# Moving nine depthwise-convolution taps of the second layer from VectorE to ScalarE, GpSimd and transfers

## The chip, the cores and the metric

The kernel runs on one core of a Trainium2 chip. The metric is the device time of one execution in microseconds. Before the change it is 2174.63 us, the median of three runs (2174.32 to 2175.8).

The engines, by the names that the profile uses: PE is TensorE (PEld its weight loads), DVE is VectorE, ACT is ScalarE, POOL is GpSimd and SP is SyncE, which issues transfers. Each engine runs its own instructions in the order in which they stand in the program, and waits on semaphores for the others.

## What is computed

An encoder trunk of two layers on 1024 tokens of width 1024, in float32. Each layer runs multi-head latent attention and a Conformer convolution side by side on the same normalised input, projects both back, and then runs a gated feed-forward block with a short convolution. Cut to what matters here:

```python
for l in range(DEPTH):                                   # DEPTH = 2
    h = _rmsnorm(x, g_mix[l])
    p = h @ w_in[l]
    c_q = _rmsnorm(p[..., :o1], g_q[l])                  # 384 wide
    q = (c_q @ w_uq[l]).reshape(b, s, 8, 96)
    c_kv = _rmsnorm(p[..., o1:o2], g_kv[l])              # 256 wide
    kv = (c_kv @ w_ukv[l]).reshape(b, s, 8, 128)
    k_rope = _apply_rope(p[..., o2:o3], cos, sin)        # 32 wide, shared by the heads
    y_attn = _mla_attention(q_nope, q_rope, k_nope, k_rope, v)
    a, gt = jnp.split(p[..., o3:], 2, axis=-1)
    u = a * jax.nn.sigmoid(gt)                           # 512 channels
    u = _dwconv(u, w_dw_conv[l], b_dw_conv[l])           # 31 taps
    u = jax.nn.silu(_layernorm(u, g_conv_ln[l], b_conv_ln[l]))
    x = x + jnp.concatenate([y_attn, u], axis=-1) @ w_o[l]
    ...                                                  # gated feed-forward block
```

`_dwconv` is the part that the change touches: for each of 512 channels, 31 shifted copies of `u`, each times a weight of its channel, are added up.

## The kernel before

Channels lie on the 128 partitions and tokens along the free dimension, so the 512 channels of the convolution are four blocks j = 0 to 3 of 128 x 1024. For each block there is a tile `gate` (which holds `u` after the gating) and a tile `conv`, in which the sum is built. One tap is one product of a shifted part of `gate` with a column of `par`, added to `conv`. The middle tap starts the sum on ACT (L693). The other 30 taps of a block are done in one of three ways:

- **near taps**, on DVE: one SCALAR_TENSOR_TENSOR multiplies and adds (L2164). `NEAR_TAPS` says how many of each block are of this kind.
- **far taps**: ACT multiplies into a tile `far` (L2170), and a transfer that POOL issues adds this tile to `conv` (L2171, 511.5 KB).
- **late taps**, during attention: POOL multiplies into a tile `late` (L2181) and either a transfer adds it (L2186) or, for every fifth, POOL itself does (kind "both", L2184). Whatever is neither near nor far becomes late.

A layer has three parts: `project`, `attention` and `feed`. `project` walks through sections of matmuls, each of which fills one PSUM bank pair: the gates and values g0, a0 to g3, a3, the key-value latents kv0 and kv1, the shared rotary key kr, the query latents q0 to q2, and from the normalised latents the keys k0 to k3, the rotary queries u0 and u1 and the other queries n0 to n3. The order of what DVE and ACT do beside them is decided while the program is written, by a model clock. After each section the clock moves on by that section's estimate, and then: if the section is longer than 5.0 us, up to `FAR_TOGETHER` far taps are put out, from blocks whose last far tap lies `FAR_GAP` = 8.0 us back; `work` fills DVE's modelled time with near taps of 1.28 us and with the steps of the evictions; and the section's own eviction is launched. So a near tap stands wherever the model saw room on DVE, and far taps stand on ACT between a section's matmuls and its eviction.

The steps of `project` that matter below, by line:

- L226 and L227 (`complete`): ACT negates a loaded weight (`wu11h` into `wu11l`), and POOL adds the original to it by a transfer, which leaves what the rounding lost. L211 is POOL's load of that weight.
- L219: ACT scales the weight of a q section.
- L756 to L771 (`key_rope`): the shared key, in turn on ACT (L756), DVE (L758, L764, L765), ACT (L768), DVE (L770) and ACT (L771).
- L304, L315 to L323, L342: the sum of squares of a latent is turned by PE, reduced and brought to a root on DVE, and turned back by PE. The key latent's root is named `rkv1`, the query's `rq1`.
- L714, L724 (`latent`): ACT brings a query latent out of PSUM into `cq` and squares it.
- L778, L780 (`key_rope_end`): the shared key split in two halves, `krs`, by ACT and DVE.
- L790, L792 (`parts`): the high half (ACT) and the low half (DVE) of a normalised latent, `kvs` or `cqs`.
- L802, L804 (`key`): the same for a key section, `ks`, out of PSUM; L804 is the last reader of its bank.
- L265: the matmuls of the sections.

Three PSUM bank pairs are used in turn, so k3 writes the bank that k0 used, k0 that of q1 and k2 that of q2. SBUF tiles of tag "b" (31 slots of 128 x 1024) take the slots that came free, whichever tile had them before; an instruction that writes a tile waits for the last reader of the slot's former one. The tiles `far` of the second layer are of tag "ws" (8 slots).

In attention each block of work goes to a step by number (`agenda`). The late taps are spread over the steps in proportion to their modelled cost. On POOL, between them, stand the heads' normalisation (`yt`, L2037), two halves `ys_1l` and `ys_3l` (L247) and at the end the sum over the four blocks (`lns`, L2192).

Of the kernel before, what the change touches and what calls it, by code (L numbers as in the profile page):

```python
# [88 lines left out]
MANUAL = [E.PE, E.DVE, E.Activation, E.Pool, E.SP]  # L89
LATE_KINDS = (("pool", "both", "pool", "pool", "pool"), ("pool", "both", "pool", "pool", "pool"))  # L90
LATE_COST = {"act": 1.1, "pool": 2.7, "both": 4.1}
NEAR_TAPS = (12, 14, 15, 14)
NEAR_ORDER = (0, 1, 2, 3)
FAR_TOGETHER = 3
FAR_GAP = 8.0
# [52 lines left out]
class Encoder:  # L148
# [442 lines left out]
    def project(self, l, carry):  # L591
# [3 lines left out]
        taps, active, u, conv, away, far_at = [], [], {}, {}, {}, {}  # L595
# [17 lines left out]
        def out_squares(now):  # L613
            while outs and outs[0][0] <= now:
                at, i, t = outs.pop(0)
                if t is None:
                    outs.append((at + OUT_WAIT, i, self.out_rows(l, i, "b")))
                    outs.sort(key=lambda e: e[0:2])
                else:
                    nc.scalar.activation(out=t, in_=t, func=AF.Square, accum_out=sc[:, 3 + i:4 + i])  # L620
# [19 lines left out]
        def work(until):  # L640
            while True:
                at = next((e for e in active if e[0] <= clock["dve"]), None)
                if at is None and taps and clock["dve"] + TAP <= until:
                    j, t = taps.pop(0)
                    self.conv_step(l, j, u[j], conv[j], t)
                    clock["dve"] += TAP
                    continue
                if at is None:
                    at = min(active, key=lambda e: e[0], default=None)
                    if at is None or at[0] > until:  # L650
                        return
                    clock["dve"] = max(clock["dve"], at[0])
                step = next(at[1], None)
                if step is None:
                    active.remove(at)
                else:
                    clock["dve"] += step[0]
                    at[0] = clock["dve"] + step[1]

        def launch(steps, n=-1):  # L660
            active.append([clock["pe"], steps, n])

        def finish(n):
            for e in [e for e in active if e[2] <= n]:
                for step in e[1]:
                    clock["dve"] = max(clock["dve"], e[0]) + step[0]
                    e[0] = clock["dve"] + step[1]
                active.remove(e)
# [17 lines left out]
        def glu(j):  # L686
            g = u[j] = gates.pop(j)
            if l:
                nc.vector.scalar_tensor_tensor(out=g, in0=ps[f"a{j}"], scalar=by, in1=g, op0=ALU.mult, op1=ALU.mult)
            else:  # L690
                nc.vector.tensor_tensor(out=g, in0=ps[f"a{j}"], in1=g, op=ALU.mult)
            y = conv[j] = self.blk(f"conv{l}_{j}")
            nc.scalar.activation(out=y, in_=g, func=AF.Identity, scale=self.tap(l, j, PAD),  # L693
                                 bias=par[:, P_BC + j:P_BC + j + 1])
            yield 1.22, 1.5
            todo = [t for t in range(KC) if t != PAD]
            taps.extend((j, t) for t in todo[:NEAR_TAPS[j]])
            taps.sort(key=lambda e: NEAR_ORDER.index(e[0]))
            away[j] = todo[NEAR_TAPS[j]:]
            far_at[j] = 0.0  # L700

        def tables():
# [188 lines left out]
        def last_gate():  # L891
            yield from glu(1)
            yield from tables()

        add("a1", "a1", inputs("a1"), last_gate)
        for j in (2, 3):
            add(f"g{j}", f"g{j}", inputs(f"g{j}"), lambda j=j: gate(j))
            add(f"a{j}", f"a{j}", inputs(f"a{j}"), lambda j=j: glu(j))
# [18 lines left out]
        times, starts, t = {}, {}, 0.0  # L917
# [12 lines left out]
        def supply(now, turn=TURN):  # L930
            for name, at in [e for e in coming if e[1] <= now + LEAD + ahead(e[0])]:
                coming.remove((name, at))
                turning.append((name, at, self.cast(l, name, "b" if l else "ws")))
            for name, at, e in [e for e in turning if e[1] <= now + turn + ahead(e[0])]:
                turning.remove((name, at, e))
                if l and name in BLOCKS:
                    e = self.scaled(*e)
                    w[name] = e[0]
                    launch(rest_of(e), st.get("n", -3) - 2)
                    continue  # L940
                w[name] = self.complete(*e)
                if name == "k":
                    head_squares(name)
# [4 lines left out]
        launch(gate(0), -3)  # L948
        work(clock["pe"] + 6.0)
        launch(glu(0), -2)  # L950
        launch(gate(1), -1)
        for n, (name, weight, emit, evict, after) in enumerate(seq):
            st["n"] = n
            supply(clock["pe"])
            out_squares(clock["pe"])
            finish(n - 3)
            if l and name == "q2":
                self.banks[0][0].append(self.banks[0][0].pop(0))
            ps[name] = self.wide(f"p{name}{l}")
            emit()  # L960
            clock["pe"] += times[name]
            queue = [i for i, _ in taps]
            far = [j for j in away if clock["pe"] >= far_at[j] and
                   (j not in queue or queue.count(j) == NEAR_TAPS[j] and queue.index(j) > 8)]
            for j in sorted(far, key=far_at.get)[:FAR_TOGETHER if times[name] > 5.0 else 0]:
                self.tap_far(l, j, away[j].pop(0), u[j], conv[j])
                far_at[j] = clock["pe"] + FAR_GAP
            work(clock["pe"])
            if after:
                after()  # L970
            launch(evict(), n)
            if l and (name[0] == "q" or name[:2] == "kv"):
                active[-1][0] += next(active[-1][1])[1]
# [1355 lines left out]
```

## Time and profile before

| | before |
|---|---|
| median of 3 runs | 2174.63 us |
| the profiled execution | 2174.99 us |
| its span, first instruction to last | 2173.2 us |
| busy share PE, DVE, ACT, POOL | 99%, 86%, 68%, 24% |
| near taps (L2164), both layers | 110, 1274 ns each |
| far taps (L2171), both layers | 31 |
| late taps (L2181), both layers | 99, 1356 ns each |

The page's rows on the busy slices of the span:

```profile
PE   9999999999999999999999999999999999999998
DVE  6989999879998887887978889998898988878877
PEclk9999999999999999999999999999999999999999
```

Each digit is the busy share of a fortieth of the span, in tenths, 9 for 90% or more; PEclk is the granted TensorE clock in the same way. The second layer's projections begin about 1120 us and end about 1283; attention follows to about 1466.

In a timeline row stand the start in us, the duration, the engine, the line, the operation, what it writes and reads, how many instructions the row groups, and in brackets how long the engine was idle before it and what ended that.

### The profile page before, as it was taken

To read this page: it belongs to the slowest core of one execution; us is meant where nothing else is said; L and a number is where in the kernel's file an instruction comes from. 1 tells how busy PE (TensorE), PEld (TensorE's weight loads), DVE (VectorE), ACT (ScalarE), POOL (GpSimd) and SP (SyncE) were. 2 spreads that over 40 slices of the span, in tenths; PEclk is the share of its full clock that TensorE was granted. 3 is DMA by queue.
4 is the path that set the end of the run, shared out by engine and by line. 5 is a ranking of instruction groups with operands and counts; after the bars stand their busy time and mean duration, and the time that the engine had idled before them with its cause. 6 is when DMAs were issued, how large, how long until landed. Compare 5 with 4: busy or idle time off the path is not lost. (4 is left out here: it accounts for less than half of the span.)

```text
span 2173.2 us, 29821 instructions
## 1 busy us (share of the span) xinstructions
PE 2160.0 (99%) x10726; PEld 1178.4 (54%) x10726; DVE 1858.7 (86%) x2558; ACT 1479.5 (68%) x2208; POOL 515.8 (24%) x506
## 2 busy tenths in 40 slices
PE   9999999999999999999999999999999999999998
PEld 8887666754444444444444576667544444444445
DVE  6989999879998887887978889998898988878877
ACT  6455888746898889554534668886478888865544
POOL 1233767211211111000001256771111111110000
PEclk9999999999999999999999999999999999999999
DMA  6898878855689898555345776786646988856533
GB/s 193 184 188 211 167 146 168 256 150 118 140 239 260 225 289 262 190 173 186 115 160 115 170 186 138 158 193 194 175 102 160 263 241 241 243 136 220 187 115 122
DMA packets 161220, 400.95 MB, mean 184 GB/s; under 512 B 19840, under 2 KB 27888, under 8 KB 161072
## 3 DMA queue, kind: packets, MB, share of 16 engines
q1 hardware_dynamic: 104080, 266.79, 35.8%
q0 software_dynamic: 56704, 131.74, 33.6%
q8 instruction: 84, 1.38, 0.3%
q14 instruction: 64, 0.52, 0.1%
q10 hardware_dynamic: 288, 0.53, 0.1%
HBM read 270.75 MB, written 69.66 MB: 157 GB/s over the span
## 5 line engine op out<-in xcount | busy, mean ns | idle before, releaser
L1384 PE MATMUL p<-b,w 128*128 128x512 f16 x3696 | 800.3, 379 | 0.2
L1384 PEld LDWEIGHTS <-w 128*128 128x128 f16 x3696 | 358.8, 98 | 431.7 <-issue 0.8
L1658 PE MATMUL pd<-ab,wd 128*128 128x512 f16 (+1 forms) x1920 | 401.0, 371 | 0.4 <-DVE ab L1648 0.4
L1260 POOL DMA_DIRECT2D wu<-in_w_up x176 | 151.8, 876 | 771.0 <-DVE w L1348 584.8
L1658 PEld LDWEIGHTS <-wd 128*128 128x128 f16 x1920 | 187.9, 98 | 210.7 <-issue 0.9
L1943 PE MATMUL s<-k,q 96*128 96x512 f16 x768 | 186.9, 379 | 0.0
L1348 DVE SCALAR_TENSOR_TENSOR w<-wu,wf,w 128x512 f16<-128x512 f32 (+1 forms) x216 | 177.1, 833 | 5.4 <-ACT w L1345 5.4
L1986 DVE SCALAR_TENSOR_TENSOR pt<-t,pt 128x512 f16<-128x512 f32 x256 | 162.9, 676 | 10.1 <-ACT pt L1985 9.1
L1345 ACT ACTIVATE w<-wu,wf 128x512 f16<-128x512 f32 (+1 forms) x216 | 164.9, 781 | 0.7 <-DMA wu<-in_w_up 0.7
L1985 ACT ACTIVATE pt<-t 128x512 f16<-128x512 f32 x256 | 139.1, 596 | 31.9 <-PE t L1983 30.0
L1945 DVE TENSOR_REDUCE mx<-s 128x1 f32<-128x1024 f32 x128 | 154.9, 1210 | 0.9 <-PE s L1943 0.9
L1647 ACT ACTIVATE ab<-ac,ds 128x512 f16<-128x512 f32 x108 | 75.5, 716 | 110.8 <-DVE ac L1553 76.2
L1953 ACT ACTIVATE p<-s,mx 128x1024 f32<-128x1024 f32 x128 | 143.3, 1119 | 2.2 <-DVE mx L1945 1.8
L2164 DVE SCALAR_TENSOR_TENSOR conv<-gate,par,conv 128x1009 f32<-128x1009 f32 (+14 forms) x110 | 139.7, 1274 | 2.8 <-ACT conv L693 0.2
L2181 POOL TENSOR_SCALAR late<-gate,par 128x1012 f32<-128x1012 f32 (+14 forms) x99 | 134.2, 1356 | 29.7 <-PE pn L265 29.7
L1983 PE MATMUL t<-ident,p 128*128 128x128 f32 x1024 | 136.6, 275 | 0.9 <-ACT p L1953 0.6
L1983 PEld LDWEIGHTS t<-ident,p 128*128 128x128 f32 x1024 | 116.8, 141 | 34.9 <-issue 7.4
L1891 DVE SCALAR_TENSOR_TENSOR o<-zg,par,o 128x1023 f32<-128x1023 f32 x88 | 112.6, 1280 | 10.0 <-ACT o L1885 8.4
L1891 DVE SCALAR_TENSOR_TENSOR v<-zv,par,v 128x1023 f32<-128x1023 f32 x88 | 112.1, 1276 | 1.4 <-ACT v L1885 1.4
L1392 DVE SCALAR_TENSOR_TENSOR zg<-p,wf,zg 128x512 f32<-128x512 f32 x72 | 54.0, 749 | 66.7 <-PE p L1384 53.0
L1943 PEld LDWEIGHTS <-q 96*128 96x128 f16 x768 | 74.1, 97 | 64.5 <-issue 2.1
L2171 POOL DMA_DIRECT2D conv<-far x31 | 27.3, 901 | 333.4 <-ACT far L2170 321.3
(1536 smaller groups left out, 3708.0 us busy)
## 6 DMA issues: line engine op xcount, KB each, us to landing
wu<-in_w_up SPq DMA_DIRECT2D x98, 512.0 KB
wu<-in_w_up POOLq DMA_DIRECT2D x176, 256.0 KB, 5.1
sd<-in_w_down SPq DMA_DIRECT2D x44, 512.0 KB
ws<-sd SPq DMA_DIRECT2D x44, 512.0 KB
act<-v SPq DMA_DIRECT2D x36, 512.0 KB
ac<-act SPq DMA_DIRECT2D x72, 256.0 KB
wo<-in_w_o POOLq DMA_DIRECT2D x32, 256.0 KB, 7.8
x_mix<-y SPq DMA_DIRECT2D x32, 256.0 KB
```

What stands on the lines that cost most here:

```text
L1260: nc.gpsimd.dma_start(out=dst, in_=src, accum_op=ALU.add)
L1345: nc.scalar.activation(out=t, in_=src, func=AF.Copy, scale=scale[f])
L1348: nc.vector.scalar_tensor_tensor(out=t, in0=src, scalar=scale[f], in1=hi, op0=ALU.mult, op1=ALU.subtract)
L1384: nc.tensor.matmul(ps, w[p][:, k * 128:(k + 1) * 128], b[:, q], start=(i in (1, 5, 2) and k == 0 and t == 0), stop=(k == 3 and t == 2), sk ...
L1658: nc.tensor.matmul(ps[t, m][:, cs], w[i, j][p][:, m * 128:(m + 1) * 128], b[:, q, cs], start=(i in (1, 5, 2) and j == 0 and s == 0), stop= ...
L1891: self.nc.vector.scalar_tensor_tensor(out=o[:, a:b], in0=z[:, at + a:at + b], scalar=self.par[l][:, tap:tap + 1], in1=o[:, a:b], op0=ALU.m ...
L1943: nc.tensor.matmul(ps[:, cs], q[0:96, i, qs], k[0:96, j, cs], start=(s == 0), stop=(s == 2))
L1945: nc.vector.tensor_reduce(out=mx, in_=ps, op=ALU.max, axis=AX.X, negate=True)
L1953: nc.scalar.activation(out=p, in_=ps, func=AF.Exp, bias=mx, accum_out=st["sums"][:, qt:qt + 1])
L1983: nc.tensor.transpose(tp[:, i, qi * 128:(qi + 1) * 128], st["p"][2 * qp + qi][:, kt * 128:(kt + 1) * 128], self.ident)
L1986: nc.vector.scalar_tensor_tensor(out=lo, in0=tp, scalar=P_SCALE, in1=hi, op0=ALU.mult, op1=ALU.subtract)
L2164: self.nc.vector.scalar_tensor_tensor(out=y[:, lo:hi], in0=u[:, lo + s:hi + s], scalar=self.tap(l, j, t), in1=y[:, lo:hi], op0=ALU.mult, o ...
```

## The change

Only numbers change: `NEAR_TAPS` becomes a tuple per layer. The first layer keeps 12, 14, 15 and 14; the second has 9, 11, 13 and 13, nine fewer. In the second layer up to four far taps follow a long section instead of three. Since far taps are put out in more and larger groups, five more taps are far there (16 before, 21 now), and the remaining four become late (49 before, 53 now).

```diff
-NEAR_TAPS = (12, 14, 15, 14)
+NEAR_TAPS = (12, 14, 15, 14), (9, 11, 13, 13)
...
-            taps.extend((j, t) for t in todo[:NEAR_TAPS[j]])
+            taps.extend((j, t) for t in todo[:NEAR_TAPS[l][j]])
...
-            away[j] = todo[NEAR_TAPS[j]:]
+            away[j] = todo[NEAR_TAPS[l][j]:]
...
-                   (j not in queue or queue.count(j) == NEAR_TAPS[j] and queue.index(j) > 8)]
-            for j in sorted(far, key=far_at.get)[:FAR_TOGETHER if times[name] > 5.0 else 0]:
+                   (j not in queue or queue.count(j) == NEAR_TAPS[l][j] and queue.index(j) > 8)]
+            for j in sorted(far, key=far_at.get)[:FAR_TOGETHER + l if times[name] > 5.0 else 0]:
```

The order of PE's and SP's instructions stays as it is. What moves on the others is shown at three places of the second layer's `project`. A far tap's name carries its block and its tap: `far_2_16` is tap 16 of block 2.

First ACT, from the weight wu01 to the start of the shared key, around section kr. Before:

```order
L226 ACTIVATE wu01l<-wu01h 128x768
L2170 ACTIVATE far_2_16_10612<-gate_2_10261,par_155 128x1023
L219 ACTIVATE wq2s<-wq21r,wz 128x1024
L226 ACTIVATE wu11l<-wu11h 128x768
L2170 ACTIVATE far_0_17_10672<-gate_0_10052,par_155 128x1022
L2170 ACTIVATE far_1_17_10675<-gate_1_10114,par_155 128x1022
L2170 ACTIVATE far_2_17_10678<-gate_2_10261,par_155 128x1022
L756 ACTIVATE krt_10682<-pkr_10579,wz 64x1024
```

The same place after:

```order
L226 ACTIVATE wu01l<-wu01h 128x768
L219 ACTIVATE wq2s<-wq21r,wz 128x1024
L226 ACTIVATE wu11l<-wu11h 128x768
L2170 ACTIVATE far_3_13_10678<-gate_3_10408,par_155 128x1022
L2170 ACTIVATE far_0_14_10681<-gate_0_10052,par_155 128x1023
L2170 ACTIVATE far_1_14_10684<-gate_1_10114,par_155 128x1023
L2170 ACTIVATE far_2_14_10687<-gate_2_10264,par_155 128x1023
L756 ACTIVATE krt_10690<-pkr_10588,wz 64x1024
```

The single far tap ahead of wq2s is gone, and four far taps instead of three stand ahead of krt.

Then POOL's issues a little earlier, which bring the weight wu11 that ACT's L226 above reads. Before:

```order
L227 DMA wu21l<-in_w_uq 128x2x384
L2171 DMA conv_0_10112<-far_0_16_10551 128x1023
L2171 DMA conv_1_10179<-far_1_16_10554 128x1023
L211 DMA wu11h<-in_w_uq 128x2x384
L227 DMA wu01l<-in_w_uq 128x2x384
```

After:

```order
L227 DMA wu21l<-in_w_uq 128x2x384
L2171 DMA conv_2_10334<-far_2_13_10557 128x1022
L2171 DMA conv_0_10112<-far_0_13_10560 128x1022
L2171 DMA conv_1_10179<-far_1_13_10563 128x1022
L211 DMA wu11h<-in_w_uq 128x2x384
L227 DMA wu01l<-in_w_uq 128x2x384
```

The load of wu11h now stands behind three far transfers instead of two.

Last DVE, around section q2, from the scale qk of the keys to the eviction of k0. Before:

```order
L636 TENSOR_SCALAR qk_9838<-qk_9838 128x1
L780 SCALAR_TENSOR_TENSOR krs_10815<-krt_10682,qk_9838,krs_10815 32x1024
L792 SCALAR_TENSOR_TENSOR kvs_0l<-ckv_10488,par_155,kvs_0h 128x1024
L792 SCALAR_TENSOR_TENSOR kvs_1l<-ckv_10566,par_155,kvs_1h 128x1024
L283 SCALAR_TENSOR_TENSOR qss_10706<-qss_10706,qss_1_10819 128x1024
L2164 SCALAR_TENSOR_TENSOR conv_3_10480<-gate_3_10402,par_155,conv_3_10480 128x1019
L2164 SCALAR_TENSOR_TENSOR conv_3_10480<-gate_3_10402,par_155,conv_3_10480 128x1020
L792 SCALAR_TENSOR_TENSOR cqs_1l<-cq_10817,par_155,cqs_1h 128x1024
L2164 SCALAR_TENSOR_TENSOR conv_3_10480<-gate_3_10402,par_155,conv_3_10480 128x1021
L2164 SCALAR_TENSOR_TENSOR conv_3_10480<-gate_3_10402,par_155,conv_3_10480 128x1022
L804 SCALAR_TENSOR_TENSOR ks_0_10924<-pk_10894,qk_9838,ks_0_10924 128x1024
```

After:

```order
L636 TENSOR_SCALAR qk_9838<-qk_9838 128x1
L792 SCALAR_TENSOR_TENSOR kvs_0l<-ckv_10494,par_155,kvs_0h 128x1024
L792 SCALAR_TENSOR_TENSOR kvs_1l<-ckv_10575,par_155,kvs_1h 128x1024
L780 SCALAR_TENSOR_TENSOR krs_10824<-krt_10690,qk_9838,krs_10824 32x1024
L283 SCALAR_TENSOR_TENSOR qss_10712<-qss_10712,qss_1_10828 128x1024
L792 SCALAR_TENSOR_TENSOR cqs_1l<-cq_10826,par_155,cqs_1h 128x1024
L804 SCALAR_TENSOR_TENSOR ks_0_10930<-pk_10902,qk_9838,ks_0_10930 128x1024
```

The four near taps ahead of the key's eviction are gone, and the two halves kvs stand ahead of krs. On ACT the same stretch keeps its order, with four far taps instead of three between L724 of q1 and L790 of cqs_1h. The slots of tag "b" are dealt out anew: L714 of q1 (cq) waited for PE before and now waits for DVE's L792 of kvs_1l, and that of kvs_0l is freed by an xs tile of section q2.

## The prediction

> **What bounds the kernel now.** I read the page first, for the engine that never rests, and then the views of the stretch that the change touches, the projections of the second layer.
>
> ```profile
> span 2173.2 us, 29821 instructions
> PE 2160.0 (99%) x10726; PEld 1178.4 (54%) x10726; DVE 1858.7 (86%) x2558; ACT 1479.5 (68%) x2208; POOL 515.8 (24%) x506
> 1120.00:1205.00 85.00, 85.00 (x402) 38.36 (x401) 77.85 (x63) 42.55 (x47) 15.88 (x17) 1.00 0.52 107
> 1205.00:1245.00 40.00, 38.26 (x188) 22.73 (x185) 30.21 (x38) 24.49 (x27) 6.56 (x8) 1.00 0.75 152
> 1283.00:1466.00 183.00, 182.57 (x1128) 110.86 (x1126) 165.29 (x216) 152.53 (x277) 132.22 (x109) 1.00 0.79 167
> ```
>
> The last three rows are windows: length, then the busy time of PE, PEld, DVE, ACT and POOL, the granted TensorE clock, the DMA share and GB/s. PE is at work throughout (85.00 of 85.00, 182.57 of 183.00) at clock 1.00; only in 1205–1245 does it lose 1.74 us. So the nine DVE taps save nothing by being fewer: time is won or lost only where PE stands still, and a shift made there is carried to the end, since PE is full behind it. The waits of PE from 1100 to 1280 (total, times, longest) name the places:
>
> ```profile
> PE pk L265 <- DVE ks L804: 1.7, 1, 1.7
> PE pu L265 <- DVE ks L804: 1.2, 1, 1.2
> PE rq1s L342 <- DVE rq1y L320: 0.7, 1, 0.7
> ```
>
> **What is to be gained.** The 1.7 is the fourth key product, k3, which writes the PSUM bank that ks_0 must leave:
>
> ```profile
> 1241.29 0.74 PE L265 MATMUL pk<-kvs_0h,wk1h 128*128 128x512 f32 x2 [1.74 <-DVE ks L804]
> 1237.25 1.09 ACT L802 ACTIVATE ks<-pk,qk 128x1024 f16<-128x1024 f32 x1
> 1233.74 2.59 DVE L2164 SCALAR_TENSOR_TENSOR conv<-gate,par,conv 128x1019 f32<-128x1019 f32 x2
> 1237.44 2.60 DVE L2164 SCALAR_TENSOR_TENSOR conv<-gate,par,conv 128x1021 f32<-128x1021 f32 x2
> 1239.96 1.28 DVE L804 SCALAR_TENSOR_TENSOR ks<-pk,qk,ks 128x1024 f16<-128x1024 f32 x1
> ```
>
> ACT had its half of ks_0 at 1237.25 + 1.09 = 1238.34; DVE began its half at 1239.96, behind four taps, all of which the change takes away here. So 1239.96 − 1238.34 = 1.62 us can go, if ACT is no later. But ACT is later, for two reasons, and PE gets a new wait before that.
>
> **Term A, a wait at 1214.6.** The chain of the shared key runs krt on ACT (L756), DVE, krt on ACT (L768), DVE L770, the norm rkv1 (to L320), and PE then turns it (L342):
>
> ```profile
> 1190.71 0.98 POOL L211 DMA_DIRECT2D wu11h<-in_w_uq  x1
> 1199.92 0.84 ACT L226 ACTIVATE wu11l<-wu11h 128x768 fp32r<-128x768 f32 x1 [0.87 <-DMA wu11h<-in_w_uq]
> 1200.67 3.21 ACT L2170 ACTIVATE far<-gate,par 128x1022 f32<-128x1022 f32 x3
> 1203.91 1.11 ACT L756 ACTIVATE krt<-pkr,wz 64x1024 f32<-64x1024 f32 x1
> 1208.97 1.05 ACT L768 COPY krt<-krt 32x1024 f32<-32x1024 f32 x1 [3.95 <-DVE krt L765]
> 1210.11 1.21 DVE L770 TENSOR_TENSOR krt<-krt,krt 32x1024 f32<-32x1024 f32 x1
> 1213.76 0.17 DVE L320 SCALAR_TENSOR_TENSOR rkv1y<-rkv1q,rkv1y 128x8 f32<-128x8 f32 x1
> 1214.62 1.04 PE L342 MATMUL rkv1s<-ident,rkv1y 128*128 128x128 f32 x8
> ```
>
> Two things come in ahead of krt. First, four far taps instead of three: one more ACTIVATE, 3.21 / 3 = 1.07. Second, ACT already waits 0.87 for the load of wu11h, so what makes that load later makes krt later by as much. POOL issues the load behind two far transfers now and behind three afterwards; the far ACTIVATE that stood between wu01l and wq2s is gone, but its time only lengthens the wait. What a third transfer costs is not in the trace, so it is bounded:
>
> ```profile
> DMA packets 215, 0.81 MB, mean 204 GB/s; under 512 B 16, under 2 KB 16, under 8 KB 215
> q0 software_dynamic: 215, 0.81, 108.2%
> 1189.06 1.89 POOL L2171 DMA_DIRECT2D conv<-far  x2 [0.88 <-ACT far L2170]
> conv<-far POOLq DMA_DIRECT2D x1, 511.5 KB, 5.5
> conv<-far POOLq DMA_DIRECT2D x1, 511.5 KB, 8.9
> wu11h<-in_w_uq POOLq DMA_DIRECT2D x1, 384.0 KB, 9.1
> ```
>
> The first two rows are the DMA view of 1192–1196, while the load waits: POOL's software queue alone is fully busy, at 204 GB/s. A far transfer is 511.5 KB = 523,776 B, so 2.57 us of that queue. Above: the two far transfers, issued at 1189.06 and some 0.95 later, landed 5.5 and 8.9 us after issue, 3.4 + 0.95 = 4.35 apart. Below: nothing, if the load is served ahead of the third transfer. I take 2.57, since the queue is full and three quarters of its time there is far data; call it L.
>
> By the Trainium skill (DMA: Bandwidth & Descriptors, section "Anatomy of one DMA — SWDGE (gpsimd) path"), a transfer issued by GpSimd takes about 2.0 us plus its bytes at 436 GB/s, which would make the third transfer worth 1.2 us. The 204 GB/s of the row above, with one queue busy, speaks against that for these accumulating transfers; by the page the whole sum below would be +2.4 instead of +3.8.
>
> So krt comes 2.57 + 1.07 = 3.64 later. The chain holds no slack up to L320: DVE's tap between L765 and L770, now gone, ended at 1210.11, but L770 also needed ACT's copy, which ended at 1210.02. Slack is only at PE: L320 ended at 1213.93, PE came at 1214.62, and PE follows DVE by 0.05 (k3 at 1241.29, ks_0's end at 1241.24), so 0.64. **A = 3.64 − 0.64 = +3.00** (L = 0 gives 0.4, L = 4.35 gives 4.8).
>
> **Term B, at k3.** These rows stand ahead of ks_0 on ACT and DVE:
>
> ```profile
> 1227.49 1.15 ACT L778 ACTIVATE krs<-krt,qk 32x1024 f16<-32x1024 f32 x1 [1.67 <-PE pq L265]
> 1228.78 1.11 ACT L714 ACTIVATE cq<-pq,wz 128x1024 f32<-128x1024 f32 x1
> 1231.00 3.21 ACT L2170 ACTIVATE far<-gate,par 128x1020 f32<-128x1020 f32 x3
> 1228.67 1.27 DVE L780 SCALAR_TENSOR_TENSOR krs<-krt,qk,krs 32x1024 f16<-32x1024 f32 x1 [2.95 <-ACT krs L778]
> 1231.40 1.28 DVE L792 SCALAR_TENSOR_TENSOR kvs_1l<-ckv,par,kvs_1h 128x1024 fp32r<-128x1024 f32 x1
> ```
>
> In the changed order the tiles of tag "b" fall on other slots: cq of q1 (ACT L714) takes the one of kv1's ckv, whose last reader is DVE's kvs_1l, so it waits for that. DVE in turn puts kvs_0l and kvs_1l ahead of krs. kvs_0l now takes the slot of an xs tile that q2 has read by about 1227.45, the one that let krs begin on ACT above (krs gets the next xs tile, some 1.3 us of PE's row later, which ends before cq can start); two L792 of 1.28 and a step between end at about 1230.1. So cq starts at 1230.1 instead of 1228.78, +1.35. The fourth far tap adds 1.07 ahead of cqs_1h and ks_0. DVE is then free when ACT's half comes, −1.62. **B = 1.35 + 1.07 − 1.62 = +0.80**; without the slot wait it is −0.55, and without the DVE gain +2.4, if DVE is held by another instruction for the 1.62. k0 and k2 also write banks that L714 frees, so part of this wait shows there; it is the same delay, not another.
>
> **What hides the rest.** Of the five far ACTIVATEs more (21 for 16), two stand in A and B. Of the others, the one ahead of cqs_0h has 3.12 us of ACT's idle time behind it (the row below), and those before 1205 lie where ACT is busy 42.55 of 85.00 us; without that cover each would cost its 1.07. In attention four more late taps cost POOL 1.36 + 0.89 each, 9.0 us:
>
> ```profile
> 1223.60 1.15 ACT L790 ACTIVATE kvs_0h<-ckv,par 128x1024 fp32r<-128x1024 f32 x1 [3.12 <-DVE ckv L735]
> L2181 POOL TENSOR_SCALAR late<-gate,par 128x1019 f32<-128x1019 f32 (+14 forms) x49 | 66.6, 1359 | 17.3 <-PE pn L265 17.3
> L2186 POOL DMA_DIRECT2D conv<-late x39 | 34.6, 887 | 12.2 <-POOL late L2181 11.6 <-DMA q<-qrd 0.3 <-PE t L1983 0.3
> L2184 POOL TENSOR_TENSOR conv<-conv,late 128x1017 f32<-128x1017 f32 (+8 forms) x10 | 24.3, 2427 | 3.1 <-DMA conv<-late 2.5
> L2037 POOL TENSOR_TENSOR yt<-yt,rb 128x1024 f32<-128x1024 f32 x3 | 7.5, 2488 | 17.8 <-DMA rb<-sd 17.8
> L247 POOL TENSOR_TENSOR ys_3l<-yt,ys_3h 128x1024 fp32r<-128x1024 f32 x1 | 2.4, 2363 | 5.0 <-ACT ys_3h L245 5.0
> ```
>
> Two of them come ahead of the 17.8 us that POOL waits, two ahead of the 5.0 (ys_3l): 4.5 of 5.0. Uncovered they would cost at most 1.0 there: if one of the two is of the kind "both", its 2.43 stands in place of 0.89, and 6.0 − 5.0 is left.
>
> **Sum:** 3.00 + 0.80 = +3.8. The profiled execution was 2174.99 us (span 2173.2 and 1.79 around it), so 2178.8 for it; it lies 0.36 above the runs' median of 2174.63, against which I forecast **2178.4**.
>
> **The rivals**, against the median. A measurement of this kernel can tell about 0.2% (4.35 us) from no change.
> - *The load is hardly held up* (L from 0 to 2.0): A 0.4 to 2.4, total +1.2 to +3.2, 2175.8 to 2177.8. For it: queues can serve transfers side by side. Against it: the full queue. 0.22.
> - *The change does what it is written for*: no later krt, no slot wait, the fourth far tap hidden, four taps gone. −1.62, 2173.0; with the slot wait alone gone and L = 0, −0.1. Against it: ACT already waits for wu11h. 0.09.
> - *Slower, through the load*: it lands one far landing later (4.35) rather than one transfer's share. A = 4.8, total +5.6, 2180.2. This decides from L = 3.1, where the total passes 4.35. For it: the landings of before are that far apart. Against it: other transfers lay between. 0.22.
> - *Faster by over 0.2%* would need PE waits of 4.35 us to go; in this stretch there are 3.6. 0.02.
>
> My own case (L 2.0 to 3.1, +3.2 to +4.3) gets 0.45. So within 0.2% 0.45 + 0.22 + 0.09 = 0.76, slower 0.22, faster 0.02. The range reaches from the −0.1 of the second rival to +5.6 and the 1.0 of POOL's tail: 2174.5 to 2181.2.
>
> **What would show it.** In the changed profile: PE waits about 3.0 for DVE rkv1y L320 where it had no wait; ACT's wait for wu11h grows by 2.57 and the time of the far ACTIVATE that was removed before it; DVE L804 follows ACT L802 at ks_0 at once; PE's waits at k0, k2 and k3 together come to 1.74 + 0.80, with ACT cq L714 among their causes; POOL still waits before ys_3l. I am wrong if PE's wait at rkv1s is under 1 or over 4.5, or if new waits of PE stand beyond 1283.

## The result and the profile after

The changed kernel takes 2178.76 us (median of 20 runs, 2177.43 to 2179.88), the kernel before 2174.49 us (20 runs, 2173.91 to 2175.8). The ratio is 1.002, 95% interval 1.0013 to 1.0027: 4.3 us or 0.2% slower. The forecast was 2178.4 in a range from 2174.5 to 2181.2.

The 20 runs fall in two groups: ten from 2177.43 to 2178.27 and ten from 2179.24 to 2179.88, with nothing between. The profile is of the lower one (2177.95, span 2176.2). Its waits of PE from 1100 to 1290, in the columns of before (two of 0.3 and 0.2 at L588, the same in both kernels, are left out):

```profile
PE rkv1s L342 <- DVE rkv1y L320: 2.0, 1, 2.0
PE pk L265 <- ACT cq L714: 1.5, 1, 1.5
PE pu L265 <- DVE ks L804: 1.2, 1, 1.2
PE rq1s L342 <- DVE rq1y L320: 0.7, 1, 0.7
PE pk L265 <- DVE ks L804: 0.4, 1, 0.4
```

Both forecast places are there: a new wait for rkv1y, and at the keys a wait for ACT's cq in place of one for DVE. The wait of 1.7 for DVE's ks_0 has shrunk to 0.4, as the change meant it to. How much each place costs is read from the starts on PE. Three rows of before that were not shown (the last one is k0), then the same places after:

```profile
1208.57 1.04 PE L304 MATMUL rkv1t<-ident,kss 128*128 128x128 f32 x8
1220.81 10.52 PE L265 MATMUL pq<-xs,wq2s 128*128 128x512 f16 x48
1230.98 0.81 PE L265 MATMUL pk<-kvs_0h,wk1h 128*128 128x512 f32 x2
```

```profile
1208.17 1.04 PE L304 MATMUL rkv1t<-ident,kss 128*128 128x128 f32 x8
1216.41 1.06 PE L342 MATMUL rkv1s<-ident,rkv1y 128*128 128x128 f32 x8 [2.02 <-DVE rkv1y L320]
1222.62 10.52 PE L265 MATMUL pq<-xs,wq2s 128*128 128x512 f16 x48
1233.26 0.73 PE L265 MATMUL pk<-kvs_0h,wk1h 128*128 128x512 f32 x2
1243.95 0.74 PE L265 MATMUL pk<-kvs_0h,wk1h 128*128 128x512 f32 x2 [0.40 <-DVE ks L804]
```

From rkv1t to rkv1s PE took 1214.62 − 1208.57 = 6.05 before and 8.24 after: **+2.19 (term A)**. From q2's start to k3 it took 1241.29 − 1220.81 = 20.48 before and 21.33 after: **+0.85 (term B)**. The waits listed at the keys grow by only 0.2, from 1.7 to 1.9. The list doesn't have that k0 starts 0.47 later (10.64 after q2's start for 10.17), nor the 0.2 that PE takes longer to come up behind two waits instead of one. Of the rest, 0.3 is a wait of PE for ACT at the start of attention (t L1983 for p L1953), 0.3 before and 0.6 now. Together that is +3.3. The two profiled executions lie 3.0 apart, since PE came to rkv1t 0.40 earlier in the second (1208.17 for 1208.57). The median of the lower group, 2178.07, lies 3.6 above the kernel before, and that of the upper group 1.5 higher still.

The rows behind term A and term B on ACT and DVE:

```profile
1201.28 0.84 ACT L226 ACTIVATE wu11l<-wu11h 128x768 fp32r<-128x768 f32 x1 [3.66 <-DMA wu11h<-in_w_uq]
1202.03 4.25 ACT L2170 ACTIVATE far<-gate,par 128x1022 f32<-128x1022 f32 x4
1206.30 1.11 ACT L756 ACTIVATE krt<-pkr,wz 64x1024 f32<-64x1024 f32 x1
1230.59 1.15 ACT L778 ACTIVATE krs<-krt,qk 32x1024 f16<-32x1024 f32 x1 [2.49 <-PE pq L265]
1232.09 1.11 ACT L714 ACTIVATE cq<-pq,wz 128x1024 f32<-128x1024 f32 x1 [0.35 <-DVE kvs_1l L792]
1241.49 1.10 ACT L802 ACTIVATE ks<-pk,qk 128x1024 f16<-128x1024 f32 x1
1229.37 1.28 DVE L792 SCALAR_TENSOR_TENSOR kvs_0l<-ckv,par,kvs_0h 128x1024 fp32r<-128x1024 f32 x1 [1.38 <-PE pq L265]
1242.62 1.28 DVE L804 SCALAR_TENSOR_TENSOR ks<-pk,qk,ks 128x1024 f16<-128x1024 f32 x1 [1.80 <-ACT ks L802]
```

ACT's wait for the load grew from 0.87 to 3.66. Of these 2.79, 1.04 is the far ACTIVATE that no longer stands in front of it (4.25 − 3.21 is what one more takes), so the load came **1.75 later**. Four far ACTIVATEs then take 4.25 instead of 3.21. Further on, cq starts 9.47 after q2's start (1232.09 − 1222.62) instead of 7.97. Most of this is krs, which stands ahead of it on ACT and now waits for a later part of q2 (7.97 instead of 6.68 after q2's start); the wait for kvs_1l adds 0.35. At the keys DVE now stands idle for 1.80 until ACT brings its half of ks_0: ACT is the late one. POOL in attention:

```profile
L2181 POOL TENSOR_SCALAR late<-gate,par 128x1021 f32<-128x1021 f32 (+13 forms) x53 | 72.4, 1367 | 17.2 <-PE pn L265 17.2
L247 POOL TENSOR_TENSOR ys_3l<-yt,ys_3h 128x1024 fp32r<-128x1024 f32 x1 | 2.4, 2357 | 2.5 <-ACT ys_3h L245 2.5
```

Of the wait of 5.0 ahead of ys_3l, 2.5 is left, so the four late taps did not make it late.

### The profile page after: what moved, and what is told of

Same layout as the page of the kernel before. It is cut to its first block, busy times and chain, and to the rows that moved or that the text cites. A ratio compares the mean times of both kernels' runs of the same rounds, so it can differ in the third digit from the quotient of the medians.

```text
span 2176.2 us, 29832 instructions
## 1 busy us (share of the span) xinstructions
PE 2160.7 (99%) x10726; PEld 1178.6 (54%) x10726; DVE 1847.6 (85%) x2549; ACT 1484.7 (68%) x2213; POOL 530.5 (24%) x519
## 3 DMA queue, kind: packets, MB, share of 16 engines
q8 instruction: 84, 1.38, 0.3%
## 4 chain that ended last, share of the span: by engine, by line
PE 93%; ACT 2%; issue 2%; DVE 2%; DMA 1%; POOL 0%; SPq 0%; DVEq 0%; POOLq 0%; ACTq 0%
PE p L1384 36%; PE pd L1658 18%; PE po L1090 7%; PE s L1943 7%; PE t L1983 5%; PE o L2005 2%; PE pa L265 2%; PE pq L265 2%; PE pg L588 2%; PE pn L265 2%; PE pg L265 1%; PE o L2010 1%; PE pv L1919 1%; PE pkv L265 1%; PE pa L588 1%
## 5 line engine op out<-in xcount | busy, mean ns | idle before, releaser
L1986 DVE SCALAR_TENSOR_TENSOR pt<-t,pt 128x512 f16<-128x512 f32 x256 | 162.9, 676 | 10.4 <-ACT pt L1985 9.5
L2181 POOL TENSOR_SCALAR late<-gate,par 128x1017 f32<-128x1017 f32 (+14 forms) x103 | 140.0, 1360 | 29.6 <-PE pn L265 29.6
L1953 ACT ACTIVATE p<-s,mx 128x1024 f32<-128x1024 f32 x128 | 143.3, 1119 | 2.5 <-DVE mx L1945 2.1
L1983 PE MATMUL t<-ident,p 128*128 128x128 f32 x1024 | 136.6, 275 | 1.1 <-ACT p L1953 0.9
L1983 PEld LDWEIGHTS t<-ident,p 128*128 128x128 f32 x1024 | 116.8, 141 | 35.2 <-issue 7.4
L2164 DVE SCALAR_TENSOR_TENSOR conv<-gate,par,conv 128x1009 f32<-128x1009 f32 (+14 forms) x101 | 128.2, 1273 | 2.7 <-ACT conv L693 0.2
L1891 DVE SCALAR_TENSOR_TENSOR o<-zg,par,o 128x1023 f32<-128x1023 f32 x88 | 112.6, 1280 | 9.9 <-ACT o L1885 8.4
(1536 smaller groups left out, 3718.9 us busy)
```

The lines of the kernel that those rows point to most:

```text
L1891: self.nc.vector.scalar_tensor_tensor(out=o[:, a:b], in0=z[:, at + a:at + b], scalar=self.par[l][:, tap:tap + 1], in1=o[:, a:b], op0=ALU.m ...
L1983: nc.tensor.transpose(tp[:, i, qi * 128:(qi + 1) * 128], st["p"][2 * qp + qi][:, kt * 128:(kt + 1) * 128], self.ident)
L1986: nc.vector.scalar_tensor_tensor(out=lo, in0=tp, scalar=P_SCALE, in1=hi, op0=ALU.mult, op1=ALU.subtract)
```

## The experiments

Theory: term A is the load's lateness plus one far ACTIVATE ahead of krt; term B is a slot wait and one far ACTIVATE, less four near taps. Rivals stand with each run. All were timed beside the kernel before on the same chip, and differences are to its median there: 2175.04 for the first four that are told, 2174.82 for the two that changed nothing, both orders right and the last group late, 2174.68 for the others. The 95% interval of such a difference reaches some 2 us to either side, so the smaller ones are read from the traces and not from the times.

**The changed kernel again.**

> The changed kernel once more, for a second profile: its 20 runs fall in two groups, about 2178.0 and 2179.6 us, and the one profile shown (2177.95) is of the lower group. Theory: the groups differ in when the load of wu11h lands, so a profile of the upper group has PE waiting about 3.5 us for rkv1y L320 where the lower has 2.0. Rival: the groups differ behind 1283 us, in attention, where POOL has less room; then PE's wait for rkv1y is 2.0 in both.

2179.55 us, five runs from 2178.22 to 2178.64 and six from 2179.55 to 2181.91. Its profile is of the upper group (2180.23), and PE waits 2.1 there, not 3.5: the load landed as in the lower group. Behind 1283 the waits of PE are those of the lower group too (0.6 at t L1983). So neither theory holds. What differs stands directly behind the wait; the last section shows it.

**The load first.** POOL's load is put ahead, and with it wu11l comes ahead of wq2s on ACT; both stood ahead of krt already.

```diff
             clock["pe"] += times[name]
+            if l and name == "kv1":
+                e = next(e for e in coming if e[0] == "u1")
+                coming.remove(e)
+                turning.append((*e, self.cast(l, "u1", "b")))
```

> Only POOL's load of wu11h is put ahead of the three far transfers behind which it stands. Theory (the load held up, plus one far ACTIVATE of 1.04): ACT no longer waits for wu11h, krt L756 starts about 0.9 us earlier than in the kernel before, PE's wait of 2.0 for rkv1y is gone, and the time falls by 2.0 to about 2176.0 for the lower group of the changed kernel (2175.4 plus what remains at k2 and k3), with no second group. Rival 1 (only the fourth far ACTIVATE matters): 0.4 of the wait would stand in for all of it already, so the load's move changes nothing and 2.0 stays. Rival 2 (more transfers slow everything by contention): the wait shrinks only in part, and the load lands no earlier than 1200.

2176.00 us (+1.0), ten of eleven runs within 0.8, no second group. The profile is of the eleventh (2177.45), which is late ahead of this stretch: rkv1t starts at 1209.85. From there to rkv1s PE takes 6.05, as in the kernel before, and it no longer waits for rkv1y. ACT:

```profile
1198.17 0.83 ACT L226 ACTIVATE wu11l<-wu11h 128x768 fp32r<-128x768 f32 x1
1204.92 1.11 ACT L756 ACTIVATE krt<-pkr,wz 64x1024 f32<-64x1024 f32 x1
```

The wait for the load is gone and the four far taps still stand ahead of krt, so the load's place behind a third transfer was needed for term A. Rivals 1 and 2 fall. One number was missed: measured from rkv1t, krt starts 0.3 earlier than in the kernel before (4.93 ahead of it for 4.66), not 0.9, since ACT now waits 0.60 for PE ahead of wq2s.

**krt first.** Section kr's eviction takes its first step at once, ahead of wu11l and the far taps of section q0. Cut to the lines that move it:

```diff
+            first = l and name == "kr"
...
-            if l and (name[0] == "q" or name[:2] == "kv"):
+            if l and (name[0] == "q" or name[:2] == "kv") or first:
                 active[-1][0] += next(active[-1][1])[1]
```

> ACT's copy of the shared key (krt L756) is put ahead of wu11l and the four far taps; POOL's order and the late load stay. Theory: the load is still late, but nothing of the shared key's chain waits for it: PE's wait of 2.0 for rkv1y is gone, time about 2176.0 as with the load first. Rival (the chain is late because of DVE or the transfers, not because of ACT's order): the wait stays at 1 us or more.

2175.83 us (+0.8), all eleven runs within 0.7. The load is still late (ACT waits 1.07 for it), krt starts at 1198.38, and PE's wait for rkv1y is gone (6.05 from rkv1t to rkv1s again):

```profile
1198.38 1.11 ACT L756 ACTIVATE krt<-pkr,wz 64x1024 f32<-64x1024 f32 x1 [1.33 <-PE pkr L856]
1201.74 0.84 ACT L226 ACTIVATE wu11l<-wu11h 128x768 fp32r<-128x768 f32 x1 [1.07 <-DMA wu11h<-in_w_uq]
```

So it is ACT's order that lets the load reach PE. What is left in both traces is term B (waits of 1.5 and 0.4 at the keys) and the 0.3 at the start of attention; the times, +0.8 and +1.0, fit.

**krs first.** DVE's order of before, by a later modelled time for the low halves kvs.

```diff
-            yield [next(p) for p in both][0]
+            yield [next(p) for p in both][0] if l == 0 else ([next(p) for p in both][0][0], 3.5)
```

> DVE's order around krs and kvs is put back to that of the kernel before (krs L780 ahead of kvs L792), so cq of q1 waits for PE's xs tile again and not for kvs_1l. The four far taps and the late load stay. Theory: PE's waits at k2 and k3 (1.5 + 0.4, and 0.1 at k0) fall by 1.35 to about 0.6, the time by 1.35 against the changed kernel; PE's wait of 2.0 for rkv1y stays. Rival (the fourth far ACTIVATE alone makes ACT late at k2): the waits stay at about 1.9.

2177.79 us, again in groups, 1.8 below the changed kernel's 2179.55 beside it. The medians of two such kernels move with the share of each group, so the waits and the starts decide:

```profile
PE rkv1s L342 <- DVE rkv1y L320: 2.3, 1, 2.3
PE pk L265 <- ACT cq L714: 0.5, 1, 0.5
PE pk L265 <- DVE ks L804: 0.4, 1, 0.4
```

```profile
1224.50 10.53 PE L265 MATMUL pq<-xs,wq2s 128*128 128x512 f16 x48
1232.47 1.11 ACT L714 ACTIVATE cq<-pq,wz 128x1024 f32<-128x1024 f32 x1
1244.45 0.73 PE L265 MATMUL pk<-kvs_0h,wk1h 128*128 128x512 f32 x2 [0.40 <-DVE ks L804]
```

At the keys 1.9 became 0.9, and from q2's start to k3 PE takes 19.95 instead of 21.33: 1.38 less, as the slot wait was priced (1.35). cq starts 7.97 after q2's start, as in the kernel before. The run puts back the slots of krs and of cq together, so it prices both and doesn't tell them apart.

**Two that changed nothing.** Both were meant to vary the far taps ahead of krt, but were written for section kr; those taps belong to section q0, and after kr none are put out. The instruction order stayed that of the changed kernel, so they count as two more measurements of it.

> After section kr three far taps are put out instead of four (the fourth becomes a late tap); the load of wu11h stays behind three transfers. Theory: the shared key is late by the load alone, 1.8, so PE's wait for rkv1y is 1.8 - 0.64, about 1.1, and the granted clock doesn't fall after so short a wait: one group of times, 2.4 above the kernel before. Rival (the late load alone makes the wait, the ACTIVATE is hidden): wait 2.0, two groups as in the changed kernel.

> The changed kernel with the first far ACTIVATE ahead of krt done twice (the same values written again), 1.04 more on ACT ahead of krt. Theory with the clock: PE's wait for rkv1y grows to about 3.1, after it the granted clock is 0.5 for some 3.4 us in every run, which costs 1.7; so one group of times, 3.4 + 1.04 + 1.7 = 6.1 above the kernel before. Rival (the two groups have another cause): two groups again, each 1.04 later, 4.4 and 6.0 above.

2179.78 us (four runs from 2178.16 to 2178.60, seven from 2179.67 to 2180.43) and 2179.58 us (four to 2178.70, seven from 2179.44 to 2181.09). With the other two measurements, 23 runs in the lower group and 30 in the upper.

**The same two for section q0.**

```diff
+[:FAR_TOGETHER + l - (l and name == "q0") if times[name] > 5.0 else 0]
```

> After section q0, whose far taps are those ahead of krt, three far taps instead of four; the fourth, far_2_14, goes one group later and the last group's far_2_17 becomes a late tap. The load of wu11h stays behind three transfers. Theory: the shared key is late by the load alone, 1.8, PE's wait for rkv1y is 1.8 - 0.64, about 1.1, and the clock stays at 1.0 after so short a wait: one group of times, 2.4 above the kernel before. Rival (the late load alone makes the wait, the ACTIVATE is hidden): wait 2.0 to 2.3, two groups at 3.6 and 5 above.

2176.83 us (+2.15), all eleven runs within 0.6. ACT and PE:

```profile
1202.42 3.21 ACT L2170 ACTIVATE far<-gate,par 128x1022 f32<-128x1022 f32 x3
1205.66 1.11 ACT L756 ACTIVATE krt<-pkr,wz 64x1024 f32<-64x1024 f32 x1
```

```profile
PE rkv1s L342 <- DVE rkv1y L320: 1.0, 1, 1.0
```

One far ACTIVATE less took 1.0 of the wait: of term A's 2.19, 1.0 is the fourth tap and the other 1.2 the load (1.75 less the slack of 0.64 is 1.1).

And the first of the four far ACTIVATEs done twice:

```diff
+                self.tap_far(l, j, away[j].pop(0), u[j], conv[j], 2 if l and name == "q0" and j == 3 else 1)
```

> The changed kernel with the first of the four far ACTIVATEs ahead of krt done twice, 1.04 more on ACT ahead of krt. Theory with the clock: PE's wait for rkv1y is about 3.1, the granted clock is 0.5 for 3.4 us behind it in every run, which costs 1.7; one group of times, 3.6 + 1.04 + 1.7 = 6.3 above the kernel before. Rival (the fall of the clock hangs on something else than the length of the wait): two groups again, 4.6 and 6.3 above.

2181.00 us (+6.3) from eight runs: two at 2179.18 and 2179.37, six from 2180.53 to 2182.26. The profile is of the lower pair: PE waits 3.5 and the clock stays at 1.00 all the same. So the length of the wait alone doesn't decide, and the rival is right in that. Whether a longer wait makes the upper group likelier is not shown: six of eight runs here, 30 of 53 with the shorter wait.

**Both orders right.** krt first and krs first together.

> Both orders put right at once: krt ahead of wu11l and the four far taps on ACT, krs ahead of kvs on DVE; all taps as in the changed kernel. Theory: term A is gone and term B is left without its slot wait, 1.07 - 1.62, so 0.4 to 0.6 below the kernel before. Rival (the parts aren't additive, a third chain takes over): no better than with krt alone, 0.8 above.

2174.57 us, −0.25, ratio 1.0000 (0.9991 to 1.0009). The parts fit (PE's waits at the keys are 0.6 and 0.4, and there is none for rkv1y). The time can't be told from that of the kernel before, so the sign of the forecast −0.4 to −0.6 is not shown. With all its taps as in the changed kernel, this version costs none of the 4.3.

**The last far group late.** As both orders right, and the four far taps of section q2 go behind u1. Cut to the expression that changes:

```diff
-[:FAR_TOGETHER + l if times[name] > 5.0 else 0]
+[:0 if l and name == "q2" else FAR_TOGETHER + l if times[name] > 5.0 or l and name == "u1" else 0]
```

> As with krt and krs first, and the last group of four far taps is put behind section u1 instead of q2, so that nothing of it stands ahead of cqs_1h, cq of q2 and ks_0. Theory: ACT's half of ks_0 comes over 3 us earlier, PE's waits from k0 to k3 are gone, and the tile of ks_1 no longer waits for k3: PE's 1.74 and up to 1.2 at u0 are won, 1.7 to 2.9 below the kernel before. Rival (the wait moves on): the chain of rq1 or the transfers at the start of attention takes the gain back, and the time stays within 0.5 of the kernel before.

2172.09 us, −2.7, ratio 0.9987 (0.9978 to 0.9996). PE waits for nothing from k0 to u0; what is left in the stretch:

```profile
PE rq1s L342 <- DVE rq1y L320: 1.4, 1, 1.4
```

The wait did move on, from 0.7 to 1.4, but kept only a part.

**The old taps in that order.**

```diff
-NEAR_TAPS = (12, 14, 15, 14), (9, 11, 13, 13)
+NEAR_TAPS = (12, 14, 15, 14), (12, 14, 15, 14)
```

With it go three far taps at a time, as in the kernel before.

> The kernel before's numbers of taps (12, 14, 15, 14 and three far taps at a time) in the order of the last experiment: krt ahead of wu11l, the last far group behind section u1. Theory: DVE's four near taps still stand ahead of ks_0, so k3 waits for DVE as before (1.7 to 2.1) though ACT is ready 3 us earlier; the time is that of the kernel before within 0.5. Then the nine taps are worth 2.7 once ACT's order is right. Rival (the order alone brings the gain): 2.2 or more below the kernel before, no wait at k3.

2174.60 us, −0.1, and the old wait is back:

```profile
PE pk L265 <- DVE ks L804: 1.7, 1, 1.7
PE pu L265 <- DVE ks L804: 1.2, 1, 1.2
```

So the order alone brings nothing to be seen, the taps alone lose 4.3, and both together win 2.7.

**The root earlier.** As with the last far group late, and rq1t behind k2.

```diff
-        between = {2 + l: lambda: root("qss", "qroot", QL, "rq")}
+        between = {2: lambda: root("qss", "qroot", QL, "rq")}
```

> The version with the last far group behind u1, and the turn of the query latent's sum of squares (rq1t) put behind k2 instead of k3, so that DVE's root stands ahead of the evictions of k2 and k3. Theory: rq1y is ready some 2 us earlier, PE's wait of 1.4 for it is gone, 4.1 below the kernel before. Rival (ks_1 or u0 becomes late, since its tile and DVE now wait for rq1t): the wait moves to u0, no better than 2.7 below.

2170.43 us, −4.25, ratio 0.9981 (0.9972 to 0.9990): the fastest of all, 8.5 below the changed kernel when each is taken against the kernel before. PE has no wait left between 1100 and 1280 over 0.4.

## Why the prediction was right, and where it was not

- **What bounds the kernel, and what the nine taps are worth.** Right. DVE's busy time fell from 1858.7 to 1847.6 us, PE's didn't (2160.0 and 2160.7), and what moved came from PE's waits. The gain at ks_0 was there: with the last far group late, PE no longer waits at k3, and u0's wait is gone as well.
- **Term A.** Right in mechanism and place, shown by the load first, krt first and three far taps. Mis-sized: +2.19 against +3.00. The step that failed is L, the price of the third transfer: 1.75 where I took 2.57 (1.75 + 1.04 − 0.64 = 2.15). The order in the queue was as assumed. The load's packets, of 1536 B each, come only behind the far data: in the row of 1192–1196 in the prediction the only packets under 2 KB are 16 under 512 B, so all of its data is far data, not three quarters; after, from 1192 to 1199, it is the same. Sixteen such small packets close each of these transfers. The load's own sixteen, before (windows 1197.92 to 1198.4 and 1199.3 to 1199.4), then after (1200.1 to 1200.6 and 1200.8 to 1200.9):

```profile
DMA packets 52, 0.06 MB, mean 119 GB/s; under 512 B 15, under 2 KB 52, under 8 KB 52
DMA packets 8, 0.01 MB, mean 108 GB/s; under 512 B 1, under 2 KB 8, under 8 KB 8
```

```profile
DMA packets 95, 0.12 MB, mean 246 GB/s; under 512 B 15, under 2 KB 95, under 8 KB 95
DMA packets 15, 0.02 MB, mean 215 GB/s; under 512 B 1, under 2 KB 15, under 8 KB 15
```

  Fifteen of the sixteen come 2.2 later, or 2.6 with the 0.40 by which PE is ahead there: the price that I took. The last one, behind which ACT goes on, lagged the others by 1.0 before and by 0.3 after. In the ten other profiles with three transfers ahead of the load it lags by 0.2 to 0.7, in the one other with two (the old taps in that order) by 1.15. So the load as a whole comes only 1.75 later: what the sum left out is that a part of it was late already, for a cause that stays open. The estimate of 1.2 us from the figures of the Trainium skill (DMA: Bandwidth & Descriptors, "Anatomy of one DMA — SWDGE (gpsimd) path") is 0.55 below the 1.75, and 2.57 is 0.82 above it.
- **Term B.** +0.85 against +0.80. The slot wait was priced at 1.35 and measured at 1.38 (krs first); the fourth far tap took 1.04, and DVE follows ACT at ks_0 at once, as worked out. On ACT cq's own wait for kvs_1l shows as 0.35 only, because krs, itself 1.29 later, stands ahead of it for the rest.
- **What hides the rest.** Right for POOL, with more to spare than forecast (2.5 of 5.0 left instead of 0.5). Missed: 0.3 more wait at the start of attention, whose cause stays open.
- **A term that the sum lacked.** A + B + 0.3 = 3.3 gives the lower group only, and 0.3 short of its median. In 30 of 53 runs of this kernel 1.5 more comes in, the clock behind the new wait, which the prediction did not have. The median stands 0.36 above the forecast because a term too large by 0.8 and a missing one of some 0.85 on average (1.5 in 30 of 53) nearly cancel. The place and the sign were argued; that the number came so near was partly luck.
- **The rivals.** By its size, 1.75, the load fell in the first rival's range (L up to 2.0, 0.22) and not in my own (2.0 to 3.1), though not for the rival's reason, since the load's bytes came behind the far data. The total of 4.3 came into my own range of +3.2 to +4.3 by the clock. The change doing what it is written for needed ACT's order as well.

## What to carry to other kernels

Work taken off an engine that isn't the bound is worth only the wait that it stood in front of, and where it goes to it stands in front of something else: look at what is queued behind it on the new engine, and what every load issued behind it is needed for. Here the same nine taps lose 4.3 us or take part in a gain of 2.7, by where the far taps stand on ACT. Once such a wait is gone, look for the next one in the chain: here ks_1's tile went with the first, and the root behind it took the gain from 2.7 to 4.25.

## What the runs showed of the hardware

The two groups are the TensorE clock. From the first profile of the upper group (the changed kernel again), PE behind its wait, and three windows of 3.41 us (the last three numbers are the granted clock, the DMA share and GB/s):

```profile
1216.92 1.75 PE L342 MATMUL rkv1s<-ident,rkv1y 128*128 128x128 f32 x8 [2.11 <-DVE rkv1y L320]
1224.81 10.52 PE L265 MATMUL pq<-xs,wq2s 128*128 128x512 f16 x48
```

```profile
1213.71:1217.13 3.42, 1.31 (x8) 0.53 (x6) 2.83 (x10) 2.88 (x4) 0.00 (x0) 1.00 1.06 207
1217.13:1220.54 3.41, 3.41 (x13) 2.01 (x12) 0.00 (x0) 2.85 (x5) 0.00 (x0) 0.50 0.02 2
1220.54:1223.95 3.41, 3.41 (x18) 1.69 (x17) 0.00 (x0) 3.41 (x4) 2.77 (x4) 1.00 0.64 119
```

After a window in which PE was busy for 1.31 of 3.41 us the clock was 0.50 for exactly one window, which costs up to half of it, 1.7: from rkv1s to q2's start PE takes 7.89 here and 6.21 in the lower group's profile. In all 14 profiles of this case the edges at which the clock rose or fell lie a whole number of 3.413 us apart, 355 of them from the first rise to this fall. Laid on the same grid, the lower group's profile of the changed kernel and that of the doubled ACTIVATE:

```profile
1211.99:1215.41 3.42, 2.40 (x12) 0.88 (x9) 2.87 (x6) 2.13 (x4) 0.00 (x0) 1.00 1.06 208
1215.41:1218.82 3.41, 2.41 (x16) 1.61 (x17) 0.71 (x5) 3.36 (x5) 0.00 (x0) 1.00 0.43 84
```

```profile
1213.14:1216.55 3.41, 1.41 (x7) 0.44 (x5) 2.43 (x4) 2.12 (x4) 0.00 (x0) 1.00 1.07 210
1216.55:1219.96 3.41, 1.90 (x13) 1.41 (x14) 1.16 (x7) 3.36 (x5) 0.00 (x0) 1.00 0.20 38
```

An edge of the grid cuts the wait in two, and the clock stays. In the three profiles in which it fell here, each of a run of the upper group, PE had been busy, by the profile's modelled times, for 1.25, 1.31 and 1.36 us of the window; at 1.41 and above it fell in none of the 14. At the end of the span, where PE runs out of work, it fell in every profile, behind a window with 0 to 1.30 us. The mean granted clock of the 53 runs, listed to three places, fits: 0.999 in all 30 of the upper group, 1.000 in 18 of the 23 of the lower. So a wait of 2 us costs 2 us or 3.5, by where the grid lies, which differs from run to run (the first rise stands 4.3 to 10.4 us into the span); a wait of 1.0 (three far taps) made no second group in eleven runs. The Trainium skill (TensorE: Matmul & The Clock Gate, "What's actually happening") has the free-running window of 3413 ns, and the traces agree with that; it has the clock fall after a window that is idle, and here a window that was busy for four tenths was enough.
